# Masked softmax on one core: one 2 MiB tile per batch, in place, with the mask on the exponent and the sums from the activation

## The chip, the cores and the metric

The kernel runs on one core of one Trainium2 chip. The metric is device time in microseconds (us). VectorE is called DVE, ScalarE ACT, GpSimd POOL and SyncE SP; SP only issues transfers here. TensorE isn't used.

## What is computed

For each of 16 batches there is a length, and each of the 8 x 256 rows of 256 numbers gets a softmax over its first `length` entries; the rest of the row is zero.

```python
x: (16, 8, 256, 256) float32, lengths: (16,) integers from 128 to 255
result = zeros_like(x)
for b in range(batch):
    length = lengths[b]
    masked = x[b, :, :, :length]
    masked = masked - max(masked, axis=-1)
    exp_masked = exp(masked)
    result[b, :, :, :length] = exp_masked / sum(exp_masked, axis=-1)
```

Input and output are 33.55 MB each. Neither kernel subtracts the row maximum, which does not change the quotient.

## The kernel before

A batch has 2048 rows. Each of the 128 partitions takes 16 rows in a row (`ntiles`), and a batch is done in two chunks of 8 rows (`chunk`), so a tile is 128 x 8 x 256 floats, 1 MiB, and there are 32 chunks.

Ahead of the loop DVE makes a 0/1 mask of 256 columns for each batch (L52, 16 instructions), from a ramp of column numbers (L40, L42) and the lengths (L45, L48). Then, for each chunk: SP issues the load of `x_tile` (L68); ACT takes the exponential of one row of 256 at a time into a second tile `exp_t` (L75, 8 instructions); DVE multiplies each of these rows by the mask and sums it (L80, 8 times; in the trace each is two instructions, the product and a read of the accumulator into `row_sum`); DVE inverts the 8 sums (L92) and multiplies the whole tile by them (L94, one instruction over 2048 elements a partition); SP issues the store (L100).

`x_tile` and `exp_t` have 6 buffers each (the pool `work`, `bufs=6`). A scheduler puts the instructions of each engine in an order; every engine then runs its list in that order and waits where a semaphore says so. All big transfers, loads and stores, are issued from SP's one list, so a load that stands behind a store in that list is issued after it, and the store's issue waits for L94. Transfers take turns on eight semaphores, and a transfer waits for the one eight places ahead of it to land.

The lines that the change touches are L60 to L102 of the loop and the set-up above it.

Of the kernel before, what the change touches and what calls it, by code (L numbers as in the profile page):

```python
# [1 line left out]

# [4 lines left out]


@with_exitstack  # L10
def kernel(
    ctx: ExitStack,
    tc: tile.TileContext,
    x: bass.AP,
    lengths: bass.AP,
    out: bass.AP,
):
    nc = tc.nc
    P = nc.NUM_PARTITIONS

    batch, heads, seq_q, seq_k = x.shape
    assert seq_k <= 512

    rows = heads * seq_q
    ntiles = rows // P
    assert rows % P == 0

    x_f = x.rearrange("b h q k -> b (h q) k").rearrange(
        "b (p t) k -> b p t k", p=P
    )  # L30
    out_f = out.rearrange("b h q k -> b (h q) k").rearrange(
        "b (p t) k -> b p t k", p=P
    )

    singles = ctx.enter_context(tc.tile_pool(name="singles", bufs=1))
    work = ctx.enter_context(tc.tile_pool(name="work", bufs=6))
    small = ctx.enter_context(tc.tile_pool(name="small", bufs=8))

    iota_i32 = singles.tile([P, seq_k], mybir.dt.int32)
    nc.gpsimd.iota(iota_i32, pattern=[[1, seq_k]], base=0, channel_multiplier=0)  # L40
    iota_f32 = singles.tile([P, seq_k], mybir.dt.float32)
    nc.vector.tensor_copy(out=iota_f32, in_=iota_i32)  # L42

    len_bcast = singles.tile([P, batch], mybir.dt.int64)
    nc.sync.dma_start(out=len_bcast, in_=lengths.partition_broadcast(P))  # L45
    len_i32 = len_bcast.bitcast(mybir.dt.int32)
    len_f32 = singles.tile([P, batch], mybir.dt.float32)
    nc.vector.tensor_copy(out=len_f32, in_=len_i32[:, ::2])  # L48

    mask01_all = singles.tile([P, batch, seq_k], mybir.dt.float32)  # L50
    for b in range(batch):
        nc.vector.tensor_scalar(  # L52
            out=mask01_all[:, b, :],
            in0=iota_f32,
            scalar1=len_f32[:, b : b + 1],
            scalar2=None,
            op0=mybir.AluOpType.is_lt,
        )

    chunk = 8  # L60
    assert ntiles % chunk == 0
    nchunk = ntiles // chunk

    for b in range(batch):
        mask01 = mask01_all[:, b, :]
        for c in range(nchunk):
            x_tile = work.tile([P, chunk, seq_k], mybir.dt.float32)
            nc.sync.dma_start(  # L68
                out=x_tile, in_=x_f[b, :, c * chunk : (c + 1) * chunk, :]
            )  # L70

            exp_t = work.tile([P, chunk, seq_k], mybir.dt.float32)
            row_sum = small.tile([P, chunk], mybir.dt.float32)
            for t in range(chunk):
                nc.scalar.activation(  # L75
                    out=exp_t[:, t, :],
                    in_=x_tile[:, t, :],
                    func=mybir.ActivationFunctionType.Exp,
                )
                nc.vector.tensor_tensor_reduce(  # L80
                    out=exp_t[:, t, :],
                    in0=exp_t[:, t, :],
                    in1=mask01,
                    scale=1.0,
                    scalar=0.0,
                    op0=mybir.AluOpType.mult,
                    op1=mybir.AluOpType.add,
                    accum_out=row_sum[:, t : t + 1],
                )

            inv_sum = small.tile([P, chunk], mybir.dt.float32)
            nc.vector.reciprocal(out=inv_sum, in_=row_sum)  # L92

            nc.vector.tensor_mul(  # L94
                out=exp_t,
                in0=exp_t,
                in1=inv_sum[:, :, None].to_broadcast([P, chunk, seq_k]),
            )

            nc.sync.dma_start(  # L100
                out=out_f[b, :, c * chunk : (c + 1) * chunk, :], in_=exp_t
            )  # L102


# [1 line left out]
_INS = ['x', 'lengths']  # L106
_OUTS = [((16, 8, 256, 256), 'float32')]


# [23 lines left out]
```

## Time and profile before

| | |
|---|---|
| median of 3 runs | 200.6 us (200.0 to 200.98) |
| profiled execution, first to last instruction (span) | 198.4 us |
| median less span | 2.2 us |
| DVE busy | 172.0 us, 87% |
| ACT busy | 82.5 us, 42% |
| DMA | 67.19 MB, mean 339 GB/s, 87% busy |

The profiled execution's time is given as its span; what lies around the span is taken as the 2.2 us by which the median exceeds it. A view that lists an instruction's start and its duration lets two neighbours overlap, so the time that one of them costs in a run of its kind is the distance from start to start, and that is shorter than the duration.

### The profile page before, as it was taken

What the parts mean: (1) busy time and instruction counts of PE and PEld (TensorE: products, weight loads), DVE (VectorE), ACT (ScalarE), POOL (GpSimd) and SP (SyncE); (2) the same over time, 40 slices, a digit from 0 to 9 for tenths busy, and PEclk for the clock granted to TensorE, in tenths of its full rate; (3) what the DMA queues carried; (4) which work ended last, traced back from release to release, by engine and by line L of the source; (5) the groups of instructions that cost most, each with busy time, mean ns of one, the idle gap of its engine ahead of it and who ended that gap; (6) DMA issues with size and microseconds to landing.
All of it is one profiled execution on the core that took longest, in us unless ns stands there. A gap on an engine that the chain in (4) does not pass through costs nothing.

```text
span 198.4 us, 1075 instructions
## 1 busy us (share of the span) xinstructions
DVE 172.0 (87%) x594; ACT 82.5 (42%) x257; POOL 0.5 (0%) x5
## 2 busy tenths in 40 slices
DVE  0999999999994999959997699968999599994990
ACT  2599505414404465055450563505842049412430
POOL 1000000000000000000000000000000000000000
DMA  4999999897989995999949999599994999959655
GB/s 102 421 431 408 372 406 391 266 373 261 381 272 386 424 388 220 340 385 426 388 206 358 377 428 381 220 350 390 400 396 193 375 380 377 401 201 393 253 211 211
DMA packets 9368, 67.19 MB, mean 339 GB/s; under 512 B 1168, under 2 KB 1168, under 8 KB 1168
## 3 DMA queue, kind: packets, MB, share of 16 engines
q1 hardware_dynamic: 9360, 67.13, 87.2%
q14 instruction: 8, 0.07, 0.1%
HBM read 33.57 MB, written 33.55 MB: 338 GB/s over the span
## 4 chain that ended last, share of the span: by engine, by line
DVE 59%; DMA 19%; issue 15%; ACT 3%; SPq 1%; ACTq 0%
DVE exp_t L80 37%; DMA x_tile<-in_x_dram 18%; DVE exp_t L94 16%; ACT exp_t L75 3%; DVE inv_sum L92 2%; DVE mask_all L52 2%; DMA len_bcast<-in_lengths_dram 2%; DVE row_sum L80 1%; SPq L100 1%; DVE iota_f L42 0%; ACTq L75 0%; DVE len_f L48 0%; SPq L68 0%
## 5 line engine op out<-in xcount | busy, mean ns | idle before, releaser
L75 ACT ACTIVATE exp_t<-x_tile 128x256 f32<-128x256 f32 x256 | 81.2, 402 | 107.0 <-DMA x_tile<-in_x_dram 76.4
L80 DVE CUSTOM_DVE_ANT_0 exp_t<-exp_t,mask_all 128x256 f32<-128x256 f32 x256 | 91.0, 417 | 15.5 <-ACT exp_t L75 15.4
L94 DVE TENSOR_TENSOR exp_t<-exp_t,inv_sum 128x2048 f32<-128x2048 f32 x32 | 73.2, 2289 | 0.8
L80 DVE DVE_READ_ACCUMULATOR2_ANT row_sum<- 128x1 f32 x256 | 20.6, 80 | 0.0
L92 DVE RECIPROCAL inv_sum<-row_sum 128x8 f32<-128x8 f32 x32 | 6.4, 200 | 0.8
L52 DVE TENSOR_SCALAR mask_all<-iota_f,len_f 128x256 f32<-128x256 f32 x16 | 4.3, 345 | 0.0
L48 DVE CAST len_f<-len_bcast 128x16 f32<-128x16 int32 x1 | 0.2, 174 | 4.4 <-DMA len_bcast<-in_lengths_dram 4.4
L75 ACT ACT_TABLE_LOAD x1 | 1.3, 1283 | 0.7 <-PEq L117 0.7
L40 POOL IOTA iota_i<- 128x256 int32 x1 | 0.3, 342 | 0.4 <-PEq L128 0.4
L42 DVE CAST iota_f<-iota_i 128x256 f32<-128x256 int32 x1 | 0.3, 284 | 0.0
L117 POOL MEMSET const-uint8-127<- 128x1 uint8 x1 | 0.1, 103 | 0.0
L117 POOL MEMSET const-bfloat16-1.0<- 128x1 bf16 x1 | 0.1, 102 | 0.0
L117 POOL MEMSET const-float32-0.0<- 128x1 f32 x1 | 0.1, 100 | 0.2 <-issue 0.2
L117 POOL MEMSET const-float32-1.0<- 128x1 f32 x1 | 0.1, 100 | 0.0
## 6 DMA issues: line engine op xcount, KB each, us to landing
x_tile<-in_x_dram SPq DMA_DIRECT2D x32, 1024.0 KB, 7.0
out_dram<-exp_t SPq DMA_DIRECT2D x32, 1024.0 KB, 4.8
len_bcast<-in_lengths_dram SPq DMA_DIRECT2D x1, 16.0 KB, 3.7
```

The lines of the kernel that those rows point to most:

```text
L40: nc.gpsimd.iota(iota_i32, pattern=[[1, seq_k]], base=0, channel_multiplier=0)
L42: nc.vector.tensor_copy(out=iota_f32, in_=iota_i32)
L48: nc.vector.tensor_copy(out=len_f32, in_=len_i32[:, ::2])
L52: nc.vector.tensor_scalar(out=mask01_all[:, b, :], in0=iota_f32, scalar1=len_f32[:, b : b + 1], scalar2=None, op0=mybir.AluOpType.is_lt,)
L75: nc.scalar.activation(out=exp_t[:, t, :], in_=x_tile[:, t, :], func=mybir.ActivationFunctionType.Exp,)
L80: nc.vector.tensor_tensor_reduce(out=exp_t[:, t, :], in0=exp_t[:, t, :], in1=mask01, scale=1.0, scalar=0.0, op0=mybir.AluOpType.mult, op1= ...
L92: nc.vector.reciprocal(out=inv_sum, in_=row_sum)
L94: nc.vector.tensor_mul(out=exp_t, in0=exp_t, in1=inv_sum[:, :, None].to_broadcast([P, chunk, seq_k]),)
L100: nc.sync.dma_start(out=out_f[b, :, c * chunk : (c + 1) * chunk, :], in_=exp_t)
L117: nc = _bacc.Bacc("TRN2", target_bir_lowering=False, num_devices=1)
```

## The change

- A tile is now a whole batch, 128 x 16 x 256 floats (2 MiB), and everything is done in it in place; there are 12 such buffers. The first 12 loads stand at the head of SP's list, and the last four, for batches 12 to 15, are issued behind the stores of batches 2 to 5. A load or store is 2 MiB in place of 1 MiB, so there are 16 of each in place of 32.
- The lengths are loaded from ACT's queue in place of SP's.
- The 16 masks are gone. For each batch DVE makes `cap`, a row of 256 numbers, (column + 0.5 - length) times -1e30: hugely positive inside the length, hugely negative outside. A `min` of the tile with `cap` (L80 of the new kernel, two instructions a batch over 2048 elements each) leaves the numbers inside the length as they are and makes the exponential of the others zero.
- The exponential (L87) also gives the sum of its row through the activation's accumulator, so the product with the mask and its sum on DVE (L80 of the old kernel) are gone.
- The product with the inverted sum is now one `tensor_scalar` for each row of 256 (L95, 16 a batch) in place of one `tensor_tensor` for each chunk (L94).

```diff
-    work = ctx.enter_context(tc.tile_pool(name="work", bufs=6))
-    small = ctx.enter_context(tc.tile_pool(name="small", bufs=8))
+    work = ctx.enter_context(tc.tile_pool(name="work", bufs=slots))   # slots = 12, ahead = 10
+    small = ctx.enter_context(tc.tile_pool(name="small", bufs=4))
-    nc.sync.dma_start(out=len_bcast, in_=lengths.partition_broadcast(P))
+    nc.scalar.dma_start(out=len_bcast, in_=lengths.partition_broadcast(P))
+    def load(b):
+        tiles[b] = work.tile([P, nt, seq_k], F32, name="x_tile", tag="x_tile")
+        nc.sync.dma_start(out=tiles[b], in_=x_f[b])
+    for b in range(min(slots, batch)):
+        load(b)
...
-            x_tile = work.tile([P, chunk, seq_k], mybir.dt.float32)
-            nc.sync.dma_start(out=x_tile, in_=x_f[b, :, c * chunk : (c + 1) * chunk, :])
-            exp_t = work.tile([P, chunk, seq_k], mybir.dt.float32)
-            for t in range(chunk):
-                nc.scalar.activation(out=exp_t[:, t, :], in_=x_tile[:, t, :], func=Exp)
-                nc.vector.tensor_tensor_reduce(out=exp_t[:, t, :], in0=exp_t[:, t, :], in1=mask01,
-                    op0=mult, op1=add, accum_out=row_sum[:, t : t + 1])
-            nc.vector.reciprocal(out=inv_sum, in_=row_sum)
-            nc.vector.tensor_mul(out=exp_t, in0=exp_t, in1=inv_sum[:, :, None].to_broadcast(...))
-            nc.sync.dma_start(out=out_f[b, :, c * chunk : (c + 1) * chunk, :], in_=exp_t)
+        nc.vector.tensor_scalar(out=cap, in0=iota_h, scalar1=len_f32[:, b : b + 1],
+            scalar2=-1.0e30, op0=subtract, op1=mult)
+        for h in range(2):
+            nc.vector.tensor_tensor(out=t[:, s, :], in0=t[:, s, :],
+                in1=cap[:, None, :].to_broadcast([P, half, seq_k]), op=ALU.min)
+            for j in range(h * half, (h + 1) * half):
+                nc.scalar.activation(out=t[:, j, :], in_=t[:, j, :], func=EXP,
+                    accum_out=row_sum[:, j : j + 1])
+            nc.vector.reciprocal(out=inv_sum[:, s], in_=row_sum[:, s])
+            for j in range(h * half, (h + 1) * half):
+                nc.vector.tensor_scalar(out=t[:, j, :], in0=t[:, j, :],
+                    scalar1=inv_sum[:, j : j + 1], scalar2=None, op0=ALU.mult)
+        nc.sync.dma_start(out=out_f[b], in_=t)
+        n = b + ahead
+        if b >= 2 and slots <= n < batch:
+            load(n)
```

The order on the engines also changes. On DVE, in the middle of the program, a chunk before is eight pairs of product and accumulator read, with the inversion and the long product of the chunk ahead among them (here from chunk `exp_t_211` to `exp_t_235`):

```order
L80 ISA exp_t_211,row_sum_212<-exp_t_211,mask01_all_72 128x256 [waits Activation_49]
L80 ISA row_sum_212 128x1
L80 ISA exp_t_235,row_sum_236<-exp_t_235,mask01_all_72 128x256 [waits DMAHW7_49,Activation_49]
L80 ISA row_sum_236 128x1
L92 RECIPROCAL inv_sum_229<-row_sum_212 128x8 [waits DVE_49]
L80 ISA exp_t_235,row_sum_236<-exp_t_235,mask01_all_72 128x256 [waits Activation_49]
L80 ISA row_sum_236 128x1
L94 TENSOR_TENSOR exp_t_211<-exp_t_211,inv_sum_229 128x2048 [waits DVE_49]
```

Now the same place has this, for the second half of batch 6 (`x_tile_78`) to the first half of batch 8 (`x_tile_82`). "L93 ... waits Activation" is where DVE waits for the eight exponentials of a half:

```order
L93 RECIPROCAL inv_sum_353<-row_sum_352 128x8 [waits Activation_49]
L80 TENSOR_TENSOR x_tile_80<-x_tile_80,cap_391 128x2048 [waits DMAHW0_49,DVE_49]
L95 TENSOR_SCALAR x_tile_78<-x_tile_78,inv_sum_353 128x256 [waits DVE_49]
L95 TENSOR_SCALAR x_tile_78<-x_tile_78,inv_sum_353 128x256 x7
L80 TENSOR_TENSOR x_tile_80<-x_tile_80,cap_391 128x2048
L93 RECIPROCAL inv_sum_394<-row_sum_393 128x8 [waits Activation_49]
L67 TENSOR_SCALAR cap_432<-iota_h_92,len_f32_94 128x256
L95 TENSOR_SCALAR x_tile_80<-x_tile_80,inv_sum_394 128x256 [waits DVE_49]
L95 TENSOR_SCALAR x_tile_80<-x_tile_80,inv_sum_394 128x256 x7
L80 TENSOR_TENSOR x_tile_82<-x_tile_82,cap_432 128x2048 [waits DMAHW1_49,DVE_49]
```

DVE used to follow ACT on a tile; now it goes ahead of ACT (the minimum) and behind it (inversion and products) on the same tile, and the pieces of two batches alternate, in a pattern that repeats every two batches.

On SP a load and a store alternated all the way, each load at the place where a buffer of six had come free:

```order
L68 DMA x_tile_233<-in_x_dram 128x2048 [waits DMAHW1_49,Activation_49]
L100 DMA out_0_dram<-exp_t_139 128x2048 [waits DMAHW2_49,DVE_49]
L68 DMA x_tile_257<-in_x_dram 128x2048 [waits DMAHW3_49,Activation_49]
L100 DMA out_0_dram<-exp_t_163 128x2048 [waits DMAHW4_49,DVE_49]
L100 DMA out_0_dram<-exp_t_187 128x2048 [waits DMAHW5_49,DVE_49]
```

Now twelve loads come first (the last of them is the first row here), then three stores, then the last four loads between stores; `x_tile_66` is batch 0, `x_tile_219` to `x_tile_348` are batches 12 to 15:

```order
L48 DMA x_tile_88<-in_x_dram 128x4096 [waits DMAHW4_49]
L102 DMA out_0_dram<-x_tile_66 128x4096 [waits DMAHW5_49,DVE_49]
L102 DMA out_0_dram<-x_tile_68 128x4096 [waits DMAHW6_49,DVE_49]
L102 DMA out_0_dram<-x_tile_70 128x4096 [waits DMAHW7_49,DVE_49]
L48 DMA x_tile_219<-in_x_dram 128x4096 [waits DMAHW5_49,DMAHW0_49]
L102 DMA out_0_dram<-x_tile_72 128x4096 [waits DMAHW1_49,DVE_49]
L48 DMA x_tile_262<-in_x_dram 128x4096 [waits DMAHW6_49,DMAHW2_49]
L102 DMA out_0_dram<-x_tile_74 128x4096 [waits DMAHW3_49,DVE_49]
L48 DMA x_tile_305<-in_x_dram 128x4096 [waits DMAHW7_49,DMAHW4_49]
L102 DMA out_0_dram<-x_tile_76 128x4096 [waits DVE_49]
L48 DMA x_tile_348<-in_x_dram 128x4096 [waits DMAHW1_49]
L102 DMA out_0_dram<-x_tile_78 128x4096 [waits DVE_49]
```

The loads no longer wait for ACT or DVE, only for a transfer eight places ahead and, for the last four, for the store that empties their buffer. On ACT the load of the exponential's table stood at the head of the list without a wait, and now stands behind the wait for the first tile.

## Rows read from the trace of the kernel before

**Rows 1.** The page's first part: busy time, share of the span, instructions.

```profile
DVE 172.0 (87%) x594; ACT 82.5 (42%) x257; POOL 0.5 (0%) x5
```

**Rows 2.** Page, 40 slices: tenths of DMA time busy, and GB/s moved.

```profile
DMA  4999999897989995999949999599994999959655
GB/s 102 421 431 408 372 406 391 266 373 261 381 272 386 424 388 220 340 385 426 388 206 358 377 428 381 220 350 390 400 396 193 375 380 377 401 201 393 253 211 211
```

**Rows 3.** Page: the chain that ended last, share of the span by engine.

```profile
DVE 59%; DMA 19%; issue 15%; ACT 3%; SPq 1%; ACTq 0%
```

**Rows 4.** Costliest groups: busy us, mean ns of one, idle before and its releaser.

```profile
L80 DVE CUSTOM_DVE_ANT_0 exp_t<-exp_t,mask_all 128x256 f32<-128x256 f32 x256 | 91.0, 417 | 15.5 <-ACT exp_t L75 15.4
L75 ACT ACTIVATE exp_t<-x_tile 128x256 f32<-128x256 f32 x256 | 81.2, 402 | 107.0 <-DMA x_tile<-in_x_dram 76.4 <-DVE row_sum L80 14.9 <-issue 9.9
L94 DVE TENSOR_TENSOR exp_t<-exp_t,inv_sum 128x2048 f32<-128x2048 f32 x32 | 73.2, 2289 | 0.8
L80 DVE DVE_READ_ACCUMULATOR2_ANT row_sum<- 128x1 f32 x256 | 20.6, 80 | 0.0
L92 DVE RECIPROCAL inv_sum<-row_sum 128x8 f32<-128x8 f32 x32 | 6.4, 200 | 0.8
L52 DVE TENSOR_SCALAR mask_all<-iota_f,len_f 128x256 f32<-128x256 f32 x16 | 4.3, 345 | 0.0
```

**Rows 5.** Waits: who waited for whom, total us, times, longest; SPq is SP's queue.

```profile
ACT exp_t L75 <- DMA x_tile<-in_x_dram: 76.4, 15, 8.3
DVE exp_t L80 <- ACT exp_t L75: 15.4, 6, 2.7
...
SPq L100 <- DVE row_sum L80: 119.0, 22, 10.6
```

**Rows 6.** Timeline of the start, merged: start us, us, engine, instruction, count.

```profile
0.73 1.28 ACT L75 ACT_TABLE_LOAD   x1 [0.73 <-PEq L117]
0.74 0.38 SPq L45 DMA_DIRECT2D len_bcast<-in_lengths_dram  x1
...
1.17 3.42 SPq L68 DMA_DIRECT2D x_tile<-in_x_dram  x6
...
4.83 4.29 DVE L52 TENSOR_SCALAR mask_all<-iota_f,len_f 128x256 f32<-128x256 f32 x16
7.12 12.50 ACT L75 ACTIVATE exp_t<-x_tile 128x256 f32<-128x256 f32 x40 [5.11 <-DMA x_tile<-in_x_dram]
```

**Rows 7.** Windows: stretch, its length, engines' busy us, clock, DMA share, GB/s.

```profile
5.00:15.00 10.00, 10.00 (x39) 7.88 (x26) 0.00 (x0) 1.00 1.02 428
...
80.00:85.00 5.00, 3.96 (x12) 0.00 (x0) 0.00 (x0) 1.00 0.99 347
...
84.50:100.00 15.50, 13.22 (x51) 8.10 (x26) 0.00 (x0) 1.00 1.01 400
...
0.00:198.40 198.40, 171.98 (x594) 82.50 (x257) 0.55 (x5) 1.00 0.87 339
```

**Rows 8.** Timeline of DVE's first chunks: start us, us, instruction.

```profile
9.39 0.42 DVE L80 CUSTOM_DVE_ANT_0 exp_t<-exp_t,mask_all 128x256 f32<-128x256 f32 x1
9.73 0.08 DVE L80 DVE_READ_ACCUMULATOR2_ANT row_sum<- 128x1 f32 x1
9.73 0.41 DVE L80 CUSTOM_DVE_ANT_0 exp_t<-exp_t,mask_all 128x256 f32<-128x256 f32 x1
...
12.15 0.19 DVE L92 RECIPROCAL inv_sum<-row_sum 128x8 f32<-128x8 f32 x1
12.27 0.37 DVE L80 CUSTOM_DVE_ANT_0 exp_t<-exp_t,mask_all 128x256 f32<-128x256 f32 x1
...
12.57 2.28 DVE L94 TENSOR_TENSOR exp_t<-exp_t,inv_sum 128x2048 f32<-128x2048 f32 x1
14.77 0.42 DVE L80 CUSTOM_DVE_ANT_0 exp_t<-exp_t,mask_all 128x256 f32<-128x256 f32 x1
```

**Rows 9.** Timeline of the end: issue of the last store (span 198.4).

```profile
193.65 0.33 SPq L100 DMA_DIRECT2D out_dram<-exp_t  x1
```

More of the change, by code (lines that the diff above doesn't have):

```diff
@@ L7 @@
 from concourse._compat import with_exitstack
+F32 = mybir.dt.float32
+ALU = mybir.AluOpType
+EXP = mybir.ActivationFunctionType.Exp
 @with_exitstack
@@ L21 @@
     batch, heads, seq_q, seq_k = x.shape
-    assert seq_k <= 512
     rows = heads * seq_q
-    ntiles = rows // P
     assert rows % P == 0
[L28 to L33, printed above, removed]
-    singles = ctx.enter_context(tc.tile_pool(name="singles", bufs=1))
-    work = ctx.enter_context(tc.tile_pool(name="work", bufs=6))
-    small = ctx.enter_context(tc.tile_pool(name="small", bufs=8))
+    nt = rows // P
@@ new lines @@
+    x_f = x.rearrange("b h q k -> b (h q) k").rearrange("b (p t) k -> b p t k", p=P)
+    out_f = out.rearrange("b h q k -> b (h q) k").rearrange("b (p t) k -> b p t k", p=P)
+    slots = 12
+    ahead = slots - 2
+    singles = ctx.enter_context(tc.tile_pool(name="singles", bufs=1))
+    work = ctx.enter_context(tc.tile_pool(name="work", bufs=slots))
+    small = ctx.enter_context(tc.tile_pool(name="small", bufs=4))
+    len_bcast = singles.tile([P, batch], mybir.dt.int64)
+    nc.scalar.dma_start(out=len_bcast, in_=lengths.partition_broadcast(P))
@@ L39 @@
+    tiles = {}
+    def load(b):
[3 more added lines that the diff above has]
+        load(b)
     iota_i32 = singles.tile([P, seq_k], mybir.dt.int32)
     nc.gpsimd.iota(iota_i32, pattern=[[1, seq_k]], base=0, channel_multiplier=0)
-    iota_f32 = singles.tile([P, seq_k], mybir.dt.float32)
-    nc.vector.tensor_copy(out=iota_f32, in_=iota_i32)
-    len_bcast = singles.tile([P, batch], mybir.dt.int64)
@@ L45 @@
-    nc.sync.dma_start(out=len_bcast, in_=lengths.partition_broadcast(P))
[L46 to L50, printed above, removed]
+    iota_h = singles.tile([P, seq_k], F32)
+    nc.vector.tensor_scalar(
+        out=iota_h, in0=iota_i32, scalar1=0.5, scalar2=None, op0=ALU.add
+    )
+    len_f32 = singles.tile([P, batch], F32)
@@ L51 @@
+    nc.vector.tensor_copy(out=len_f32, in_=len_bcast.bitcast(mybir.dt.int32)[:, ::2])
     for b in range(batch):
+        t = tiles.pop(b)
+        cap = small.tile([P, seq_k], F32, name="cap", tag="cap")
         nc.vector.tensor_scalar(
-            out=mask01_all[:, b, :],
-            in0=iota_f32,
+            out=cap,
+            in0=iota_h,
             scalar1=len_f32[:, b : b + 1],
-            scalar2=None,
-            op0=mybir.AluOpType.is_lt,
-        )
-    chunk = 8
-    assert ntiles % chunk == 0
@@ L62 @@
[L62 to L66, printed above, removed]
-            x_tile = work.tile([P, chunk, seq_k], mybir.dt.float32)
-            nc.sync.dma_start(
-                out=x_tile, in_=x_f[b, :, c * chunk : (c + 1) * chunk, :]
-            )
-            exp_t = work.tile([P, chunk, seq_k], mybir.dt.float32)
-            row_sum = small.tile([P, chunk], mybir.dt.float32)
-            for t in range(chunk):
+            scalar2=-1.0e30,
@@ new lines @@
+            op0=ALU.subtract,
+            op1=ALU.mult,
+        )
+        row_sum = small.tile([P, nt], F32, name="row_sum", tag="row_sum")
+        inv_sum = small.tile([P, nt], F32, name="inv_sum", tag="inv_sum")
+        half = nt // 2
+        for h in range(2):
+            s = slice(h * half, (h + 1) * half)
+            nc.vector.tensor_tensor(
+                out=t[:, s, :],
+                in0=t[:, s, :],
+                in1=cap[:, None, :].to_broadcast([P, half, seq_k]),
+                op=ALU.min,
+            )
+            for j in range(h * half, (h + 1) * half):
@@ L75 @@
                 nc.scalar.activation(
-                    out=exp_t[:, t, :],
-                    in_=x_tile[:, t, :],
-                    func=mybir.ActivationFunctionType.Exp,
-                )
[L80 to L88, printed above, removed]
-                )
@@ L91 @@
-            inv_sum = small.tile([P, chunk], mybir.dt.float32)
-            nc.vector.reciprocal(out=inv_sum, in_=row_sum)
[L94 to L102, printed above, removed]
+                    out=t[:, j, :],
+                    in_=t[:, j, :],
@@ new lines @@
+                    func=EXP,
+                    accum_out=row_sum[:, j : j + 1],
+                )
+            nc.vector.reciprocal(out=inv_sum[:, s], in_=row_sum[:, s])
+            for j in range(h * half, (h + 1) * half):
+                nc.vector.tensor_scalar(
+                    out=t[:, j, :],
+                    in0=t[:, j, :],
+                    scalar1=inv_sum[:, j : j + 1],
+                    scalar2=None,
+                    op0=ALU.mult,
+                )
+        nc.sync.dma_start(out=out_f[b], in_=t)
```

## The prediction, made before the changed kernel ran

> **What bounds the kernel now.** I read the busy times first: DVE is busy 172.0 of 198.4 us [rows 1], so it is the engine that sets the pace, but not alone. The chain that ended last gives DVE 59%, DMA 19% and "issue" 15% [rows 3]. The groups show where DVE's time goes: the product with the mask 91.0 us, its accumulator read 20.6, the long product with the inverted sums 73.2; and it stands idle 15.5 us ahead of L80, for ACT [rows 4]. The waits show why: ACT itself waits 76.4 us for loads, while SP's queue stands 119.0 us in front of stores that wait for DVE [rows 5]. A load behind such a store in SP's list is issued only when DVE has caught up, and lands late. The slices show the same: DMA runs at 9 tenths for a stretch, then has a slice at about 200 GB/s [rows 2]. Read as one loop: DVE late, store late, next load late, ACT late, DVE idle.
>
> **How fast can the transfers go?** Whatever the change does, 67.1 MB must move. The first stretch has loads alone, at 428 GB/s; loads and stores mixed with DMA fully busy move 400, and the worst full slice that I found 347; over the whole span it is 339 with a DMA share of 0.87 [rows 7]. 339/0.87 = 389 GB/s is what all busy time gives, mixed.
>
> *Transfers after.* Half a megabyte moves in the first 4.96 us [rows 2], so the first byte moves near 3.8 us. The first big load was then issued at 1.17, behind the lengths' at 0.74 [rows 6]; it now heads SP's list, so about 3.3. Twelve loads, 25.2 MB at 428: 58.8 us, to 62.1. Then S0 S1 S2 L12 S3 L13 S4 L14 S5 L15, of which nine (18.9 MB) alternate or stand at a turn; at 400, 47.2 us. The other eleven transfers are stores in a row, 23.1 MB. No row shows a long run of stores alone; the ends are 428 (as loads) and 389, and I take 428, since the slow stretches are the mixed ones: 53.9 us. Sum 163.2 us. This holds if the stores are ready in time: the stores of batches 0 to 5 are computed before 62 us, and a batch of DVE work (below, 9.2 us) against a transfer (4.9) means that DVE is caught up with only at the end.
>
> **DVE after, part by part.**
> *Removed*: 256 products with their reads, 345 ns from start to start (9.39 to 9.73) [rows 8], so 88 us; 32 long products at 14.77 - 12.57 = 2.20 us [rows 8], 70 us; 16 masks at 4.29/16 = 0.268 us [rows 6]; 32 inversions.
> *Added*, for a batch: two minima over 2048 elements. The row closest is L94, also two float32 operands with one of them broadcast: 2 x 2.20 = 4.40. Sixteen products of 128 x 256 with a scalar per partition: the row is L52, the same instruction in shape and type, 0.268 from start to start: 16 x 0.268 = 4.29. Its duration, 345 ns [rows 4], is the upper bound, if neighbours should not overlap. Two inversions at 12.27 - 12.15 = 0.12 [rows 8]; one `cap` at 0.27. Sum 4.40 + 4.29 + 0.24 + 0.27 = 9.2 us a batch, 147.2 for 16. Before it was 2 x (8 x 0.345 + 0.12 + 2.20) = 10.2 a batch. So DVE is relieved by little; most of the gain is that nothing has to wait.
>
> *Start and end.* ACT began at 7.12 on the first 1 MiB [rows 6]. The load of 2 MiB takes 2.45 us more (1.05 MB at 428), less 0.43 for the earlier issue: DVE begins at 9.1. The lengths, `cap` and the ramp come before that and hide behind it. The table load, 1.28 us [rows 6], now follows the first tile and hides behind the first minimum, 2.20. At the end the last store: 198.4 - 193.65 = 4.8 us for 1 MiB [rows 9], and 2.45 more: 7.2. DVE path: 9.1 + 147.2 + 0.3 (last exponentials) + 7.2 = **163.8 us**, if DVE never waits. The two paths end within a microsecond of each other.
>
> **The cost that no row shows: the accumulator on ACT.** An exponential without a sum costs (12.50 - 0.40)/39 = 0.310 us from start to start [rows 6]. Call its pace with the sum a. On DVE a sum adds an instruction of 80 ns [rows 4], which starts together with the next product, so it costs no pace of its own [rows 8]. Ends: a = 0.31 (as on DVE) and 0.62 (the read costs as much as another exponential). Between: the read waits for the tail of its own exponential (402 - 310 = 92 ns) and then takes 80: 0.48. A gain is excluded, since work is added.
>
> Is ACT covered? From the order shown with the change, the pattern repeats every two batches (78 and 80 there), 2 x 9.2 = 18.4 us of DVE without waits. Two loops go through both engines. *Loop A* starts when the first-half minimum of 78 ends: ACT does the 16 exponentials of 78 (16a, and 0.2 for the two tails), DVE then inverts and makes 80's first minimum (0.12 + 2.20, hence 2.3), and from there its list has 2.14 of products, 2.20, 0.12, 0.27, 2.14 and 2.20 until the first minimum of 82, which is where 78 began: 9.1. Together 11.7 + 16a. *Loop B* is ACT's: 32 exponentials in a row, but for one gap of inversion, minimum and tails a period: 2.5 + 32a. The period is the longest of 18.4, A and B, and there are 8. A passes 18.4 at a = 0.42. With 0.31 the period is 18.4; with 0.48 it is 19.4, 8 us in all; with 0.62, 22.3, 31 us.
>
> I take a = 0.44, near the middle between overlapped and waiting for its tail, leaning to the latter because ACT's tail (92 ns) is the longer one (DVE's is 417 - 345 = 72 [rows 4, 8]). Period 18.74: +2.7. DVE path 163.8 + 2.7 = 166.5, above the transfers' 163.2.
>
> **Sum.** 166.5 us span, against 198.4. The runs' median is 2.2 above the span before; with that 168.7. Forecast **168.5 us**.
>
> **Rivals.**
> 1. *The accumulator takes ACT's time in full.* For it: no row shows it, and ACT's own list now waits for DVE at every half. With a = 0.48 the time is 163.8 + 8 + 2.2 = 174; with 0.55 (period 20.5) 183; with 0.62, 197. Against: DVE's read overlaps.
> 2. *Transfers are the bound at mixed rates.* With 389 GB/s after the loads: 62.1 + 41.9/0.389 = 170 + 2.2 = 172. With 347 throughout that stretch: 62.1 + 121 + 2.2 = 185. For it: the 347 slice. Against: the same trace holds 400 to 428 over 10 and 15 us. The Trainium skill (DMA: Bandwidth & Descriptors, Specifications) puts a core's HBM limit at about 358 GB/s; by that, an estimate from the page, the transfers alone would need 187 us, about 193 in all. The trace disagrees, with 428 GB/s over 10 us and 400 over 15.5 [rows 7], and the skill's HBM Reference (Specifications (TRN2)) allows about 425 to a core that streams alone.
> 3. *The products don't overlap*, 345 instead of 268 ns: 256 x 0.077 = 19.7 more, 163.8 + 19.7 + 2.2 = 186. Against: L52 ran 16 in a row at 268.
> 4. *Slower than before*: exponential and read run one after the other, each to its end and with ACT's full start, 402 + 309 = 0.71 us. ACT alone then needs 182 us, and by loop B the period is 25.2, 54 us above 18.4: 163.8 + 54 + 2.2 = 220. It decides from a = 0.63, where the time passes 200.6. Place: L87, every instruction. Against it: nothing on either engine of this trace runs that unoverlapped.
> 5. *It does not do what it says*: were a tile's halves tied together, so that DVE and ACT took turns on a half, 32 x (2.20 + 8 x 0.31 + 0.4 + 2.14) = 231 us, some 250 with start, last store and the 2.2. The order speaks against it: the second half's minimum has no wait for ACT, and another tile's work stands between.
>
> **How the numbers follow.** Forecast (a up to 0.46, transfers at 400 or better; 164 to 171): 0.50. Rival 1 below 0.63: 0.27. Rival 2: 0.13. Rival 3: 0.05. Rival 4: 0.04. Rival 5: 0.01. The range 163.5 to 183 holds the forecast, rival 1 up to a = 0.55 and most of rival 2, some 8 in 10. Its low end: with a = 0.31 DVE's path gives 166.0, five of the 16 `cap` rows (1.35) are ahead of the first tile in DVE's list and may cost nothing, and the transfers at 428 throughout end at 3.3 + 156.8 = 160.1, 162.3 with the 2.2; that is no bound. A difference of 0.5% is about what a measurement of this kernel can tell from none; all cases but 4 and 5 lie far below it, and rival 1 touches the time before only at its end (0.01): faster 0.94, same 0.01, slower 0.05.
>
> **What would show it.** Right: DVE busy near 150 us with few waits for ACT; the first 60 us of slices at 420 GB/s; then stores back to back with no slice at 200; ACT's rows with a pace of 0.31 to 0.46. Wrong: a second ACT row of 256 with a mean above 100 ns and DVE's inversion (L93) waiting for L87 more than 5 us in all (rival 1, 4); slices below 400 GB/s at full DMA share after 110 us, where stores stand alone (rival 2); L95 at 345 from start to start (rival 3).

## The result

The changed kernel takes 166.41 us in the median (165.88 to 166.48) against 200.3 for the kernel before in the same measurement: a ratio of 0.8297, interval 0.8272 to 0.8321. The forecast was 168.5, with 163.5 to 183. The profiled execution has a span of 164.7 us, forecast at 166.5. One of the four runs of e12 below (203.3 us) was a slow one and is not in its ratio.

The page of the changed kernel, its busy times and its 40 slices (to be held against [rows 1, 2]; a slice is now 4.1 us):

```profile
DVE 145.0 (88%) x338; ACT 105.9 (64%) x513; POOL 0.5 (0%) x5
...
DVE  0059999999999999999999999999999999999600
ACT  0038999177977476937887676937694887857200
...
DMA  5999999999999999999999999999999999999693
GB/s 168 333 411 418 442 436 426 424 426 434 426 422 438 434 416 426 442 434 422 422 434 432 434 428 414 434 438 418 426 442 438 418 428 440 430 438 418 287 390 139
```

DVE and DMA are now both at 9 tenths from the fourth slice to the 37th. The slices of about 200 GB/s that came back again and again before [rows 2] are gone; the only dip, 287 in the 38th slice, is taken up under e2.

Its costliest groups (busy us, mean ns of one, idle before), the counterpart of [rows 4]:

```profile
L87 ACT ACTIVATE x_tile<-x_tile 128x256 f32<-128x256 f32 x256 | 102.5, 402 | 37.9 <-issue 23.3
L80 DVE TENSOR_TENSOR x_tile<-x_tile,cap 128x2048 f32<-128x2048 f32 x32 | 72.0, 2253 | 0.0
L95 DVE TENSOR_SCALAR x_tile<-x_tile,inv_sum 128x256 f32<-128x256 f32 x256 | 69.6, 339 | 0.1
L87 ACT ACTIVATION_READ_ACCUMULATOR x_tile<-x_tile 128x1 f32 x256 | 47.8, 187 | 0.0
L61 DVE CAST len_f<-len_bcast 128x16 f32<-128x16 int32 x1 | 0.2, 174 | 9.9 <-DMA len_bcast<-in_lengths_dram 9.9
...
L93 DVE RECIPROCAL inv_sum<-row_sum 128x8 f32<-128x8 f32 x32 | 5.9, 186 | 1.0 <-ACT x_tile L87 1.0
```

DVE's idle time for ACT was 15.4 us ahead of L80 [rows 4] and is now 1.0 in all, at the very end of the program. It waits once more, at the start: 9.9 us for the lengths. The sum on ACT is an instruction of its own, 187 ns long. What it costs in pace is seen where ACT runs without a break (timeline: start us, us):

```profile
13.58 0.40 ACT L87 ACTIVATE x_tile<-x_tile 128x256 f32<-128x256 f32 x1
13.89 0.19 ACT L87 ACTIVATION_READ_ACCUMULATOR x_tile<-x_tile 128x1 f32 x1
13.98 0.40 ACT L87 ACTIVATE x_tile<-x_tile 128x256 f32<-128x256 f32 x1
```

From 13.58 to 13.98 is 0.40 us for a row, 0.31 for the exponential and 0.09 for the read. So a = 0.40. The two loops of the prediction put the point from which DVE waits at 0.42.

### The profile page after: what moved, and what is told of

Its sections match the earlier page's. It is cut to its first block, busy times and chain, and to the rows that moved or that the text cites. A ratio compares the mean times of both kernels' runs of the same rounds, so it can differ in the third digit from the quotient of the medians.

```text
span 164.7 us, 981 instructions
## 1 busy us (share of the span) xinstructions
DVE 145.0 (88%) x338; ACT 105.9 (64%) x513; POOL 0.5 (0%) x5
## 4 chain that ended last, share of the span: by engine, by line
DVE 86%; DMA 6%; ACT 2%; issue 1%; DVEq 0%; ACTq 0%
DVE x_tile L80 42%; DVE x_tile L95 39%; DMA len_bcast<-in_lengths_dram 6%; DVE inv_sum L93 2%; ACT x_tile L87 2%; DVE cap L67 2%; DVEq L131 0%; DVE iota_h L57 0%; DVE len_f L61 0%; ACTq L131 0%
## 5 line engine op out<-in xcount | busy, mean ns | idle before, releaser
L87 ACT ACTIVATE x_tile<-x_tile 128x256 f32<-128x256 f32 x256 | 102.5, 402 | 37.9 <-issue 23.3
L80 DVE TENSOR_TENSOR x_tile<-x_tile,cap 128x2048 f32<-128x2048 f32 x32 | 72.0, 2253 | 0.0
L95 DVE TENSOR_SCALAR x_tile<-x_tile,inv_sum 128x256 f32<-128x256 f32 x256 | 69.6, 339 | 0.1
L87 ACT ACTIVATION_READ_ACCUMULATOR x_tile<-x_tile 128x1 f32 x256 | 47.8, 187 | 0.0
L93 DVE RECIPROCAL inv_sum<-row_sum 128x8 f32<-128x8 f32 x32 | 5.9, 186 | 1.0 <-ACT x_tile L87 1.0
L67 DVE TENSOR_SCALAR cap<-iota_h,len_f 128x256 f32<-128x256 f32 x16 | 4.7, 309 | 0.0
```

What stands on the lines that cost most here:

```text
L67: nc.vector.tensor_scalar(out=cap, in0=iota_h, scalar1=len_f32[:, b : b + 1], scalar2=-1.0e30, op0=ALU.subtract, op1=ALU.mult,)
L80: nc.vector.tensor_tensor(out=t[:, s, :], in0=t[:, s, :], in1=cap[:, None, :].to_broadcast([P, half, seq_k]), op=ALU.min,)
L87: nc.scalar.activation(out=t[:, j, :], in_=t[:, j, :], func=EXP, accum_out=row_sum[:, j : j + 1],)
L93: nc.vector.reciprocal(out=inv_sum[:, s], in_=row_sum[:, s])
L95: nc.vector.tensor_scalar(out=t[:, j, :], in0=t[:, j, :], scalar1=inv_sum[:, j : j + 1], scalar2=None, op0=ALU.mult,)
```

## The experiments

Times are medians; ratios are to the kernel before, measured beside each. In the code shown, lines are joined to save space and `...` marks what is left out.

| run | what | us | ratio, interval |
|---|---|---|---|
| changed kernel | | 166.41 | 0.830 (0.827 to 0.832) |
| e1 | its transfers, no work | 164.57 | 0.820 (0.817 to 0.824) |
| e2 | lengths first on SP | 165.97 | 0.828 (0.826 to 0.831) |
| e3 | no sums on ACT | 166.16 | 0.829 (0.825 to 0.833) |
| e4 | ACT at 0.49 us a row | 166.57 | 0.831 (0.828 to 0.835) |
| e5 | ACT at 0.585 us a row | 173.76 | 0.867 (0.864 to 0.870) |
| e6 | new transfers, old work | 186.77 | 0.932 (0.929 to 0.935) |
| e7 | old transfers, new work | 212.05 | 1.058 (1.055 to 1.061) |
| e8 | both ends cut finer | 166.30 | 0.830 (0.827 to 0.832) |
| e9 | 4 resident tiles | 186.64 | 0.931 (0.927 to 0.935) |
| e10 | transfers only, 1 MiB in turn | 164.27 | 0.819 (0.816 to 0.823) |
| e11 | transfers only, 2 MiB in turn | 165.06 | 0.824 (0.819 to 0.828) |
| e12 | kernel before, loads on ACT's queue | 198.72 | 0.986 (0.981 to 0.991) |

### What bounds the changed kernel: e1, e2, e8

**e1.** The loop over the batches keeps only the loads and stores.

```diff
     for b in range(batch):
         t = tiles.pop(b)
-        cap = small.tile([P, seq_k], F32, name="cap", tag="cap")
...
-                nc.vector.tensor_scalar(out=t[:, j, :], in0=t[:, j, :],
-                    scalar1=inv_sum[:, j : j + 1], scalar2=None, op0=ALU.mult)
         nc.sync.dma_start(out=out_f[b], in_=t)
```

> The changed kernel with all the work of DVE and ACT on the tiles left out: the same 16 loads and 16 stores in the same order on SP, the output is a copy of the input. My theory says that transfers and DVE end within a microsecond or two of each other in the changed kernel, so transfers alone should take nearly its time: 2.7 us to the first byte and 67.1 MB at 429 GB/s (156.4 us) make 159 to 162 us of span, 161 to 164 us of device time against 166.4. The rival that DVE alone sets the time and the transfers have slack would show a clearly shorter run, which 429 GB/s does not allow; the rival that stores and loads only reach 400 GB/s when nothing slows them gives 170 or more.

Measured 164.57, 0.6 above the range expected: the transfers alone take all but 1.8 us of the changed kernel's time. Slices of e1:

```profile
DMA  5999999999999999999999999999999999999992
GB/s 154 340 399 442 438 418 430 442 414 430 438 418 430 438 418 430 438 418 434 434 422 430 430 434 418 430 426 426 442 426 418 446 430 414 442 438 422 430 446 93
```

No rate is lost where the last loads stand between stores. The two rivals fall: there is hardly any slack in the transfers, and no 400 GB/s. It sets the floor for any kernel that moves these bytes with these transfers.

**e2.** One line.

```diff
-    nc.scalar.dma_start(out=len_bcast, in_=lengths.partition_broadcast(P))
+    nc.sync.dma_start(out=len_bcast, in_=lengths.partition_broadcast(P))
```

> One edit: the lengths' small load is issued on SP ahead of the tiles, as in the kernel before, in place of ACT's queue beside them. In the changed kernel it landed after 9.2 us, with the first tile, where it took 3.7 before; DVE's first minimum started at 10.85. Theory: the minimum starts when the first tile lands, near 9.0 to 9.8, and DVE's path is 1.0 to 1.8 us shorter; the tiles start 0.4 us later, so the time falls by 0.5 to 1.2 us, to 165.2 to 165.9. Rival, the transfers alone set the end: unchanged or 0.4 us longer.

Why it was tried: in the changed kernel the lengths land after 9.2 us, beside the big loads, and not after 3.7 as before. Issues of the changed kernel (KB, median us to landing), and DVE's start in it:

```profile
len_bcast<-in_lengths_dram ACTq DMA_DIRECT2D x1, 16.0 KB, 9.2
...
10.85 4.49 DVE L80 TENSOR_TENSOR x_tile<-x_tile,cap 128x2048 f32<-128x2048 f32 x2
```

In e2 the first minimum starts at 9.49, and the last store is issued at 154.32 where the changed kernel's goes out at 156.1 (its line last, with the first and last start of all its stores):

```profile
9.49 4.49 DVE L80 TENSOR_TENSOR x_tile<-x_tile,cap 128x2048 f32<-128x2048 f32 x2 [3.87 <-DMA x_tile<-in_x_dram]
...
154.32 0.33 SPq L102 DMA_DIRECT2D out_dram<-x_tile  x1
...
L102 SPq DMA_DIRECT2D out_dram<-x_tile x16: 332/333/453, 29.4 to 156.1; - x16
```

DVE's path is 1.8 us shorter, as expected. The median is only 0.44 us shorter, just under the 0.5 to 1.2 expected, and the intervals don't tell that from nothing. The last store takes 164.1 - 154.3 = 9.8 us in place of 164.7 - 156.1 = 8.6: what DVE gains at the front the transfers keep at the end.

The end itself shows which path is the longer one. Windows of the same stretch (length, engines' busy us, clock, DMA share, GB/s) in the changed kernel, in e1 and in e2:

```profile
150.00:158.00 8.00, 4.93 (x19) 3.30 (x16) 0.00 (x0) 1.00 0.79 338
...
150.00:158.00 8.00, 0.00 (x0) 0.00 (x0) 1.00 1.01 434
...
150.00:158.00 8.00, 3.23 (x13) 1.83 (x10) 0.00 (x0) 1.00 0.97 412
```

In the changed kernel the DMA engines lack work for 0.21 x 8 = 1.7 us there, around the issue of the last store; in e1 they never do, and in e2 hardly. So the changed kernel ends with DVE's path and its last store, and this gap is about the size of the 1.8 us by which it exceeds e1.

**e8** goes further: lengths first, the first load and the last store in halves of 1 MiB.

```diff
-    nc.scalar.dma_start(out=len_bcast, in_=lengths.partition_broadcast(P))
+    nc.sync.dma_start(out=len_bcast, in_=lengths.partition_broadcast(P))
...
-        nc.sync.dma_start(out=tiles[b], in_=x_f[b])
+        if b == 0:
+            for h in range(2):
+                s = slice(h * nt // 2, (h + 1) * nt // 2)
+                nc.sync.dma_start(out=tiles[b][:, s, :], in_=x_f[b, :, s, :])
+        else:
+            nc.sync.dma_start(out=tiles[b], in_=x_f[b])
...
-        nc.sync.dma_start(out=out_f[b], in_=t)
+            if b == batch - 1:
+                nc.sync.dma_start(out=out_f[b, :, s, :], in_=t[:, s, :])
+        if b < batch - 1:
+            nc.sync.dma_start(out=out_f[b], in_=t)
```

> Three edits to the changed kernel, for a better one: the lengths first on SP, the first batch's load cut into two of 1 MiB, and the last batch's store cut into two of 1 MiB, the first of them issued when its half is done. Theory: DVE starts near 7.5 in place of 10.85, and its path ends with a 1 MiB store: 7.5 + 145.3 + 5 = 158 us, so that only the transfers are left, 163 us of span in the run without work: 163.5 to 164.7 of device time. If instead something that both share sets the end, 166.

Measured 166.30, unchanged: the 163.5 to 164.7 that I expected failed, and the 166 of the alternative held. DVE does start at 7.17, but it runs dry at 14.47 for the second tile, and though its last half is done just after 154 us and the last 1 MiB follows at once, the span ends at 164.7:

```profile
7.17 4.70 DVE L85 TENSOR_TENSOR x_tile<-x_tile,cap 128x2048 f32<-128x2048 f32 x2 [2.16 <-DMA x_tile<-in_x_dram]
...
14.47 2.29 DVE L85 TENSOR_TENSOR x_tile<-x_tile,cap 128x2048 f32<-128x2048 f32 x1 [1.81 <-DMA x_tile<-in_x_dram]
...
152.27 2.19 DVE L100 TENSOR_SCALAR x_tile<-x_tile,inv_sum 128x256 f32<-128x256 f32 x8
```

A last store of 1 MiB took 4.8 us in the kernel before [rows 9]; here some 10 pass after DVE's end, so it waits behind other transfers. Together the three runs say that DVE's path, the longer one in the changed kernel, lies less than 2 us above the transfers' own, and that shortening it hands the end to the transfers, with next to nothing gained. Why e2 and e8 still end 1.2 and 1.8 us of span after e1 is not settled; up to 0.4 of it can come from their first tile, issued behind the lengths (at 1.16 us in place of 0.74).

### Is ACT hidden: e3, e4, e5

**e3** leaves the sums out; the inversion still waits for ACT, as it reads a column of the exponentials.

```diff
-                    accum_out=row_sum[:, j : j + 1],
...
-            nc.vector.reciprocal(out=inv_sum[:, s], in_=row_sum[:, s])
+            nc.vector.reciprocal(out=inv_sum[:, s], in_=t[:, s, 0])
```

> The exponentials give no sums (the accumulator is left out; the inversion takes the exponential of each row's first column in its place, so the rows are scaled wrongly and the sums are left out of the computation). DVE's inversion still waits for ACT's eight exponentials. Theory: the accumulator read costs ACT 0.09 us a row (0.40 in place of 0.31) and is hidden, since DVE begins to wait only from 0.42: the time stays at 166.4 within 1 us. Rival, ACT is on the path: 256 x 0.09 = 23 us less work on it would show as several us.

166.16, unchanged, with 48 us of accumulator reads gone from ACT, about 23 us of its pace. DVE's list has the same order as in the changed kernel, so this is a clean test: the reads are hidden.

**e4** cuts each exponential in two, only the first with a sum, so that ACT is slower.

```diff
-                nc.scalar.activation(out=t[:, j, :], in_=t[:, j, :], func=EXP,
-                    accum_out=row_sum[:, j : j + 1])
+                nc.scalar.activation(out=t[:, j, :192], in_=t[:, j, :192], func=EXP,
+                    accum_out=row_sum[:, j : j + 1])
+                nc.scalar.activation(out=t[:, j, 192:], in_=t[:, j, 192:], func=EXP)
```

> ACT is made slower and nothing else: each exponential is cut into 192 columns with the sum and 64 columns without (the last 64 columns are left out of the sums). An extra instruction costs ACT some 0.095 us, so the pace goes from 0.40 to about 0.495 us a row, above the 0.42 from which, by the two loops of the prediction, DVE waits. Theory: loop A, 11.6 + 16 x 0.495 = 19.5 us for two batches against 18.1, eight times: 10 to 12 us more, 176 to 178. Rival, ACT (64% busy) has slack and the pace does not matter before ACT is full (0.57): unchanged at 166 to 167.

166.57, unchanged: my expectation failed and the rival's held. ACT did slow down, to 0.49 us a row (80.67 less 80.18, timeline of ACT), and DVE still waits for ACT for 1.2 us only (waits: total us, times, longest):

```profile
80.18 0.34 ACT L87 ACTIVATE x_tile<-x_tile 128x192 f32<-128x192 f32 x1
80.43 0.18 ACT L87 ACTIVATION_READ_ACCUMULATOR x_tile<-x_tile 128x1 f32 x1
80.52 0.24 ACT L90 ACTIVATE x_tile<-x_tile 128x64 f32<-128x64 f32 x1
80.67 0.35 ACT L87 ACTIVATE x_tile<-x_tile 128x192 f32<-128x192 f32 x1
...
DVE inv_sum L92 <- ACT x_tile L87: 1.2, 1, 1.2
```

The reason lies in the list of DVE. With the extra instruction the scheduler wrote another order: inversion, products, the next batch's first minimum, inversion, its second minimum, products, the same for every batch. In the timeline of DVE, from a batch's first minimum to its first and second inversion:

```profile
80.41 2.28 DVE L80 TENSOR_TENSOR x_tile<-x_tile,cap 128x2048 f32<-128x2048 f32 x1
82.61 0.20 DVE L92 RECIPROCAL inv_sum<-row_sum 128x8 f32<-128x8 f32 x1
...
86.98 0.19 DVE L92 RECIPROCAL inv_sum<-row_sum 128x8 f32<-128x8 f32 x1
...
91.61 0.19 DVE L92 RECIPROCAL inv_sum<-row_sum 128x8 f32<-128x8 f32 x1
```

The minimum's place ends at 82.61, where the batch before is inverted, and the batch's own second inversion comes at 91.61, 9.0 us later; its sixteen exponentials, 7.8 us, fit in between. Loop A belongs to the order of the changed kernel alone, and as the order changed with ACT's work, this run doesn't test it.

**e5** cuts in two halves of 128 with a sum each.

```diff
...
-                nc.scalar.activation(out=t[:, j, :], in_=t[:, j, :], func=EXP,
-                    accum_out=row_sum[:, j : j + 1])
+                nc.scalar.activation(out=t[:, j, :128], in_=t[:, j, :128], func=EXP,
+                    accum_out=row_sum[:, j : j + 1])
+                nc.scalar.activation(out=t[:, j, 128:], in_=t[:, j, 128:], func=EXP,
+                    accum_out=row_sum2[:, j : j + 1])
```

> Each exponential is cut into two of 128 columns, each with its own sum (the second half's sums are left out of the inversion). From the run with one cut, ACT's pace for a row should be 2 x (0.20 + 0.09) = 0.585 us. In this kernel's order DVE makes the minima a whole batch ahead, so ACT is never short of work. Theory now, after the run with one cut: the order decides how much of ACT is covered, and ACT sets the end only when it is full: 13.2 us until it starts, 256 x 0.585 = 150, then 2.6 for the last products and 8 for the last store: 174 us of span, 175 to 176 of device time. By loop B of the prediction (2.5 + 32a = 21.2 a period against 18.1) it would be 25 us more than 166.4, 190. If transfers alone set the time it stays at 166.

173.76. ACT is busy 150.9 of 172.0 us and now heads the chain:

```profile
DVE 146.3 (85%) x338; ACT 150.9 (88%) x1025; POOL 0.5 (0%) x5
...
ACT 60%; DVE 29%; DMA 5%; issue 1%; DVEq 0%; ACTq 0%
```

That is ACT at its full pace (a little under the 175 to 176 expected), not the 190 of loop B, for in this order DVE makes its minima a batch ahead and ACT never runs dry. So a slower ACT costs nothing as far as 0.49 us a row where the order covers it, and everything from where ACT is full: 166.4 less the 24 us of start, end and surroundings that e5 has (173.8 - 150) leaves 142 us, 0.56 us a row, an estimate.

### Which half of the change did it: e6, e7, e9, e12

**e6** has the new transfers and the work of the kernel before:

```diff
...
+        nc.vector.tensor_scalar(out=mask01, in0=iota_h, scalar1=len_f32[:, b : b + 1],
+            scalar2=None, op0=ALU.is_lt)
         for h in range(2):
-            nc.vector.tensor_tensor(out=t[:, s, :], in0=t[:, s, :], in1=cap, op=ALU.min)
             for j in range(h * half, (h + 1) * half):
-                nc.scalar.activation(out=t[:, j, :], in_=t[:, j, :], func=EXP,
-                    accum_out=row_sum[:, j : j + 1])
+                nc.scalar.activation(out=t[:, j, :], in_=t[:, j, :], func=EXP)
+                nc.vector.tensor_tensor_reduce(out=t[:, j, :], in0=t[:, j, :], in1=mask01,
+                    scale=1.0, scalar=0.0, op0=ALU.mult, op1=ALU.add, accum_out=row_sum[:, j : j + 1])
...
+            nc.vector.tensor_mul(out=t[:, s, :], in0=t[:, s, :],
+                in1=inv_sum[:, s][:, :, None].to_broadcast([P, half, seq_k]))
```

> The transfers of the changed kernel (2 MiB, in place, 12 loads at the head) with the work of the kernel before: exponential without a sum, product with a 0/1 mask and its sum on DVE, one long product for half a batch. Theory: the old work needs 10.2 us of DVE a batch, 163 us, and with nothing late it runs from about 11.5 to 175, then the last store, 8: 182 to 184 us of span, 184 to 186 of device time. So about half of the 34 us would come from the transfers' order alone. Rival, the gain is DVE's lighter work: near 200. Rival, only transfers decide: 167.

186.77, just above the 184 to 186 expected. DVE now never waits for ACT or a tile once it has begun, and its own work is the bound; the transfers are done early and go idle in the last quarter of the slices:

```profile
DVE 167.7 (91%) x594; ACT 80.5 (44%) x257; POOL 0.5 (0%) x5
...
DVE  0089999999999999999999999999999999999940
ACT  2099989999998991007355271800000000000000
...
DMA  6999999999999999999999999999976190825546
```

So the transfers alone bring 200.3 - 186.8 = 13.5 of the 34 us. The other 186.8 - 166.4 = 20.4 come when DVE's lighter work is added to them: DVE is busy 145.0 us in the changed kernel and 167.7 here.

**e7** is the other half: the new work on the tiles, buffers and transfers of before.

```diff
-    slots = 12
+    slots = 6
...
-    for b in range(min(slots, batch)):
-        load(b)
...
         for h in range(2):
+            x_tile = work.tile([P, half, seq_k], F32, name="x_tile", tag="x_tile")
+            nc.sync.dma_start(out=x_tile, in_=x_f[b, :, s, :])
+            exp_t = work.tile([P, half, seq_k], F32, name="exp_t", tag="exp_t")
...
+            nc.sync.dma_start(out=out_f[b, :, s, :], in_=exp_t)
```

> The work of the changed kernel on the tiles and transfers of the kernel before: 1 MiB chunks, two tiles of six buffers each, loads issued between the stores in SP's one list, lengths first on SP. Theory: DVE has 147 us of work in place of 163, but loads stay behind stores that wait for DVE, and DVE now also waits for ACT between minimum and inversion with only six buffers to run ahead in: 180 to 195. If the lighter work were the gain and the waits no matter, 163 + 9 + 5 - 16 = 161 to 166.

212.05: 12 us slower than the kernel before, and above all that I had expected, although DVE has 24 us less to do. Its waits, and SP's list (timeline: start us, us, count):

```profile
DVE x_tile L74 <- DMA x_tile<-in_x_dram: 40.7, 8, 8.2
...
DVE inv_sum L87 <- ACT exp_t L81: 12.0, 9, 3.4
...
62.96 15.25 SPq L96 DMA_DIRECT2D out_dram<-exp_t  x5
78.30 3.69 SPq L70 DMA_DIRECT2D x_tile<-in_x_dram  x5
```

Five stores in a row, each waiting for DVE, take 15.25 us to issue, and the five loads behind them go out only then; DVE stands still for 40.7 us in all. Before, DVE waited for ACT for 15.4 [rows 5]. SP's list is not that of the kernel before, either: there one or two stores stand between two loads (the order shown with the change has such a pair at its end, so loads and stores don't strictly alternate), here the scheduler put five stores and then five loads. So the 12 us are the price of the new work together with the order that it leads to, and this run doesn't part the two. DVE now stands at both ends of a tile's way, and what runs ahead of its own stores has to be in memory already.

**e9** keeps everything but the depth.

```diff
-    slots = 12
+    slots = 4
```

> One number: 4 resident tiles in place of 12 (a load is issued two batches ahead, behind a store). The scheduler then writes another order for DVE too: both minima of a batch, then inversion and products of the same batch, with little of another batch between. Theory: depth is what the lighter work needs, for the loads and for the order alike. A batch alone takes minimum 2.2, sixteen exponentials at 0.40 (6.4), inversion and products of the second half 2.3, so some 11 us in place of 9.05: 11 x 16 + 11 + 8 = 195, more with late loads: 190 to 215. Rival, 12 buffers are more than needed and 4 keep the transfers busy: 166 to 172.

186.64, below the range that I had expected, but 20 us above 12 tiles. DVE's waits (total us, times, longest):

```profile
DVE inv_sum L93 <- ACT x_tile L87: 13.2, 15, 1.2
...
DVE x_tile L80 <- DMA x_tile<-in_x_dram: 4.0, 6, 1.1
```

DVE waits 12.2 us more for ACT and 4.0 more for tiles, and is busy 149.6 us in place of 145.0: that is the 20. The 12.2 go with the new order: in ten of the sixteen batches both minima stand together with the first inversion right behind them, and eight exponentials (3.2 us) don't fit behind one minimum of 2.2. One number altered two things, the depth and the order that the scheduler makes of it, and this run doesn't part them.

**e12** takes the kernel before and issues the loads from ACT's queue.

```diff
-            nc.sync.dma_start(
+            nc.scalar.dma_start(
                 out=x_tile, in_=x_f[b, :, c * chunk : (c + 1) * chunk, :]
             )
```

> The kernel before with one edit: the loads are issued from ACT's queue in place of SP's, so no load stands behind a store that waits for DVE. Work, tiles, buffers and transfers are those of before. The scheduler puts the loads in pairs among ACT's exponentials, behind the exponentials that free their buffers. Theory: the wait of loads behind stores was what kept DVE idle; without it DVE runs its 163 us from 9 and the last store takes 5, 177 us of span, 179 of device time. Rival, the six buffers were what held the loads back: 195 to 200.

198.72, by the ratio a gain of 1.4% (0.9 to 1.9), not 10: the theory that the place behind the stores was the whole cause falls, and the rival's 195 to 200 held. ACT still waits 46.0 us for loads and DVE 14.1 for ACT:

```profile
ACT exp_t L75 <- DMA x_tile<-in_x_dram: 46.0, 11, 5.3
...
DVE exp_t L80 <- ACT exp_t L75: 14.1, 11, 2.3
```

The loads now stand behind exponentials, and those wait for buffers that DVE and the stores have to free. That is the rival's explanation, but this run doesn't prove it: the transfers also moved only 354 GB/s at a DMA share of 0.99 between 60 and 70 us, and 29 of the 40 slices count as 9 tenths busy at 321 to 426 GB/s. At such a rate the transfers alone fill most of the time. Whether the six buffers or the rate held the loads back is open; why a busy DMA was slower with loads and stores on two queues was not tried further.

### The rate of mixed transfers: e10, e11

Loads and stores in turn, no work, 1 MiB (four loads ahead, 24 buffers) or 2 MiB (two ahead, 12 buffers). The lines shown are from e10; `tl` issues the load of one tile, and e11 has whole batches and `lead = 2`:

```diff
...
+    lead = 4
+    for i in range(lead):
+        tl(i)
+    for i in range(2 * batch):
+        b, h = divmod(i, 2)
+        nc.sync.dma_start(out=out_f[b, :, h * hf : (h + 1) * hf, :], in_=tiles[i])
+        if i + lead < 2 * batch:
+            tl(i + lead)
```

> Transfers only (all work on the tiles left out, the output is a copy of the input), in the manner of the kernel before: 1 MiB each, four loads ahead, then store, load, store, load, with nothing to wait for but the data. It asks what the 389 to 400 GB/s of mixed stretches before were. If a turn between load and store costs rate, or 1 MiB does, it takes 67.1 MB at 400 GB/s and 3 us, 171 us of span, 172 to 175 of device time; if the mixed stretches were slow because transfers were issued late, it runs at 428 like the loads and takes the 164.6 of the run without work.

> The same with 2 MiB transfers, two loads ahead and then store, load in turn. Against the run with 1 MiB it tells size from order: if size alone matters, 164 to 165; if the turns matter, twice fewer of them, half of what the 1 MiB run loses.

164.27 and 165.06: neither the turns nor the size cost anything that matters. Slices of e10, where behind the first loads every transfer is followed by one in the other direction:

```profile
GB/s 139 309 424 426 428 432 426 426 428 432 426 426 428 432 424 428 428 432 424 428 428 432 424 428 428 430 426 428 428 430 426 428 428 428 426 430 428 428 426 268
```

So the 400 GB/s of the kernel before in fully busy mixed stretches [rows 7] is no property of mixing loads and stores on one queue. What is left is that they are issued late there, in the gaps of the others. e9, with the changed kernel's transfers but loads issued late, points the same way (328 to 446 GB/s in slices that count as 9 tenths busy), but no run changed lateness alone, so this cause is argued, not shown. Why a DMA engine counts as busy there at a lower rate stays open too.

## Why the prediction was right, point by point

- **The mechanism** held: with the loads at the head the loop of late store, late load, late DVE is gone, DVE's waits fall to 1.0 us behind the start, and two paths of nearly the same length remain. But what carries it is both halves together. The new transfers alone bring 13.5 us, the new work on the old transfers costs 12, together 34. The prediction's remark that DVE "is relieved by little" and that most of the gain is "that nothing has to wait" did not hold. DVE was busy 172.0 us [rows 1] and is busy 145.0, 27.0 less, while its idle time fell from 26.4 to 19.7, by 6.7 only (the waits for ACT went, but the start and the last store grew longer); and with nothing left to wait for but with the old work (e6) 13.5 of the 34 us are won. The prediction's own prices say so as well: 16 x 10.2 + 4.3 for the masks is 20 us more than 147.2.
- **Transfers, 163.2 us**: e1's span is 162.9. The total came out by luck, with a wrong term in it: nine transfers were taken at 400 GB/s and ran at 428 or more, so that this term was 3.1 us too long. It is made up mostly at the end, which the sum left out: in e1 (window as above) hardly any engine is still at work from 160 us on, and the span ends 2.9 us later. The start costs 0.4 us (the first three slices carry 3.64 MB, where 428 GB/s from 3.3 us on would carry 3.8).

```profile
160.00:162.00 2.00, 0.00 (x0) 0.00 (x0) 1.00 0.08 33
```

- **DVE's batch, 9.2 us**: from the chain of the changed kernel, minima of the same place two batches apart start at 80.64 and 98.64 (the last line is from the timeline):

```profile
80.64 2.20 DVE x_tile L80
...
98.64 2.20 DVE x_tile L80
...
78.46 2.17 DVE L95 TENSOR_SCALAR x_tile<-x_tile,inv_sum 128x256 f32<-128x256 f32 x8
```

  9.0 a batch. Rival 3 (products that don't overlap) is out: eight products take 2.17 us together, close to the 8 x 0.268 that L52 gave.
- **DVE's start, 9.1 us**: the step that failed. "The lengths, `cap` and the ramp come before that and hide behind it" took the 3.7 us of a small load that is alone. Issued beside the big ones it took 9.2, and with the ramp and two rows of `cap` behind it the first minimum began at 10.85. It cost 1.7 us on DVE's path, and e2, which takes 1.4 of them back, is next to nothing faster.
- **The last store, 7.2 us**: 8.6. It did find the queue nearly free, as the sum had it: when it was issued, at 156.1, the DMA share was down to 0.08. Its 2 MiB move from 156.5 to 161.5, the 4.9 us of the sum; then work for one or two of the 16 engines goes on until 163 (windows of the changed kernel):

```profile
155.50:156.00 0.50, 0.50 (x2) 0.00 (x0) 0.00 (x0) 1.00 0.08 33
...
161.50:162.00 0.50, 0.00 (x0) 0.00 (x0) 0.00 (x0) 1.00 0.09 33
162.00:162.50 0.50, 0.00 (x0) 0.00 (x0) 0.00 (x0) 1.00 0.15 66
162.50:163.00 0.50, 0.00 (x0) 0.00 (x0) 0.00 (x0) 1.00 0.08 33
```

  Why some of the engines end later than the rest no run shows.
- **The accumulator**: a = 0.44 was taken, 0.40 measured, inside the bounds of 0.31 and 0.62; the 2.7 us for it were not spent. The read does not wait for the exponential's tail and then cost its full length (0.48), nor is it free, as the prediction took DVE's to be. Of the sign that the prediction gave for rivals 1 and 4 only the first half came, a second ACT row of 187 ns; DVE's inversion waits 1.0 us for ACT, not over 5. Without the 2.7 the sum of the DVE path was 163.8. The start took 1.7 more, the last wait 0.7 more (1.0 for 0.3), the last store 1.4 more, the work between 3.0 less (156.0 - 10.85 - 1.0 = 144.2 for 147.2): 164.6, against a span of 164.7. What lies around the span was 1.8 us and not 2.2. So the forecast is within 1.3% because errors of both signs nearly cancel; that part is luck.
- **The loops A and B** were used for the prices of rival 1. Loop A's terms add up to 11.6, not 11.7, which changes nothing here. No run had the changed kernel's order with a slower ACT, so the loops are unproved, and 190 for a pace of 0.59 was wrong for the kernel that the scheduler made of it: 173.8.
- **Rival 2** (transfers at 389, 347 or 358 GB/s): out by e1, e10 and e11. As a bound the transfers, at 428 GB/s, lie less than 2 us below the changed kernel all the same.
- **Rivals 4 and 5** did not come; the read overlaps (rival 4's 309 ns for it stand in no row; it measured 187), and the halves of a tile are apart.

## What to carry to other kernels

Run the transfers alone early: it gives the floor in one run, and here the changed kernel stands 1.1% above it, so that three more edits (e2, e3, e8) brought nothing that can be told from noise. Lighter work on an engine that both starts and ends a tile's way paid here only with the loads in memory far ahead; measure such halves together, because alone one brought 13.5 us and the other cost 12. When an experiment changes one engine's work under a scheduler, look at the order first: it may have been rewritten, and then it tests another program.

## What the runs showed of the hardware that I had not expected

- An exponential with a sum is followed by a read of 187 ns that costs 0.09 us of ACT's pace (0.40 against 0.31 us a row of 256). On DVE such a read (80 ns) starts together with the next product [rows 8]; no run left it out, so whether it costs pace there is not shown.
- A 16 KB load took 3.2 to 3.7 us at the head of the queue and 9.2 us issued at the same moment from another queue, beside loads of 2 MiB (6.1 with the loads of 1 MiB on ACT's queue, in e12).
- Loads and stores in turn on one queue move at 424 to 432 GB/s in the full slices of e10, as loads alone do.
- The DMA engines don't end together: in the changed kernel a share of about 0.1 is at work for 1.5 us after the bulk of the last store is through.
